# Gate and up products of an encoder layer: sums of weights as additions, two of four made by accumulating transfers

## The chip, the cores and the metric

One core of a Trainium2 chip runs the whole program in one launch. The metric is the device time of one execution in microseconds, lower is better. Engines are named as in the profile: PE is TensorE (matmuls), PEld its weight loads, DVE is VectorE, ACT is ScalarE, POOL is GpSimd, SP is SyncE, which here only issues transfers.

## The reference

One layer of an encoder, applied with the same weights to 512 rows (`x_sample`) and 256 rows (`x_prompt`) of 1024 float32 numbers: a mixer of attention and a gated recurrence, then a gated feed-forward part with a short convolution. The change concerns the first two products of the latter, with weights of 1024 x 2816 each:

```python
def _conv_ffn(xn, w_gate, w_up, conv_w, conv_b, w_down):
    a = xn @ w_gate
    a = lax.conv_general_dilated(a, conv_w[:, None, :], window_strides=(1,),
        padding=((CONV_WIDTH // 2, CONV_WIDTH // 2),),
        dimension_numbers=('NWC', 'WIO', 'NWC'), feature_group_count=D_FF) + conv_b
    b = xn @ w_up
    return (jax.nn.gelu(a, approximate=True) * b) @ w_down
```

## The kernel before

All 768 rows are worked on together. Every float32 operand of a matmul is kept as two float32r parts, a high part (a copy on ScalarE, line 242) and a low part (the difference on VectorE, line 243), and a product is the sum of three matmuls, high by high, high by low, low by high (`split_to`, `product`).

The gate and up products use Strassen's scheme in Winograd's form. The 1024 x 2816 weights are taken in 22 *pairs* p of column tiles: an even p is a tile f of 128 columns of gate and the tile f + 11, an odd p the same tiles of up. A pair is a 2 x 2 matrix of blocks (two halves of the 1024 inputs by the two column tiles), the token rows are halved likewise (2 x 384), and seven products P1 to P7 replace eight. `PRODS` gives their order: P1, P5, P6, P3, P7, P2, P4, each of 4 x 3 matmuls of 128 x 128 by 128 x 384 (`product`, line 857). The sums of token blocks are made once (`ffn_transpose`, lines 792 to 797). The sums of weight blocks are made for each pair: with b11, b21 the two halves of tile f and b12, b22 those of the other tile, P5 needs b12 - b11, P6 that sum taken from b22, P7 needs b22 - b12, P4 the one of P6 taken from b21. They are VectorE operations of 128 x 512 at line 841, written to one of six rotating slots of the buffer `V`.

What each product adds to is fixed by banks of PSUM (`BANK_OF`): P1, P6, P7 and P4 accumulate in one bank, P5 and P3 in a second, P2 has a third; two sets of banks alternate between pairs. In between the bank is read: `keep` (line 873, ScalarE) copies P1, P6 and P5 as they stand, `collect` (line 893, VectorE, and line 889, ScalarE) adds a kept copy to a bank and writes a part of the output. So P6 can only start when P1 has been copied, P3 when P5 has been copied, P4 when the bank has been read after P7. After an even pair follow the convolution (lines 901 to 903) and Gelu (line 904), after an odd pair the multiplication (line 908) and two stores of the gated rows to memory (lines 909 and 910).

The loop of `run` takes products m one after the other: `prep(m)`, `product(m)`, `keep(m)`, `collect(m)`, `prep(m + 6)`. `prep` makes the sum, if the product has one, and splits its weight operand into slot m mod 8 of a ring of eight (`W`), so a split waits until the product eight places earlier is done. At P4 of a pair `prep` also calls `load`, which orders the raw weights of two further tiles on SP (line 228, 512 KB each, five buffers in rotation), the second tile of pair p + 2 and the first of pair p + 3. The first four products in order are P1 and P2 of the first two pairs; then comes the rest of pair 0, pair 1 and so on.

The program is built with `manual_schedule` for SP and POOL: these two queues run in the order of the program text. The order of PE, ACT and DVE is laid down when the program is built and differs from the text (in the trace, ScalarE splits the weights of P3 of the second pair before those of P4 of the first). On the chip every queue runs in its order and waits on semaphores.

Of the kernel before, what the change touches and what calls it, by code (L numbers as in the profile page):

```python
# [10 lines left out]
OP = mybir.AluOpType  # L11
# [7 lines left out]
NF = DFF // 128  # L19
# [15 lines left out]
N_FFN = 40  # L35
# [57 lines left out]
class Encoder:  # L93
# [680 lines left out]
    def ffn_transpose(self, i):  # L774


        nc = self.nc
        b = (3, 5)[TILES.index(i) % 2]
        for k in range(NK):
            nc.tensor.transpose(self.ps[:, b + k // 4, 128 * (k % 4):128 * (k % 4) + 128],  # L780
                                self.v(self.xrow(i) + 128 * k, 128), self.ident)
        t = i % 3
        p1, p2 = self.ps[:, b, :], self.ps[:, b + 1, :]
        r1, r2 = self.V + 1024 * t, self.V + 1024 * t + 512
        if i < 3:
            for name, p, r in (("A11", p1, r1), ("A12", p2, r2)):
                self.operand_split(name, t, p)
                nc.scalar.activation(self.v(r, 512), p, AF.Copy)
            return
        ta, s1 = self.xrow(i), self.xrow(i) + 512  # L790
        nc.scalar.activation(self.v(ta, 512), p2, AF.Copy)
        nc.vector.tensor_tensor(self.v(s1, 512), p1, self.v(ta, 512), op=OP.add)
        self.operand_split("S1", t, self.v(s1, 512))
        nc.vector.tensor_tensor(self.v(ta, 512), self.v(r1, 512), p1, op=OP.subtract)
        nc.vector.tensor_tensor(self.v(r1, 512), self.v(s1, 512), self.v(r1, 512), op=OP.subtract)
        self.operand_split("S2", t, self.v(r1, 512))
        nc.vector.tensor_tensor(self.v(r2, 512), self.v(r2, 512), self.v(r1, 512), op=OP.subtract)
        self.operand_split("S4", t, self.v(r2, 512))
        self.operand_split("S3", t, self.v(ta, 512))
        self.operand_split("A22", t, p2)  # L800
# [26 lines left out]
    def prep(self, upto):  # L827

        nc = self.nc
        while self.n_op < min(upto + 1, len(self.prods)):  # L830
            m = self.n_op
            p, kind = self.prods[m]
            n = N_FFN + 2 * p
            b11, b12 = self.raw(n), self.raw(n if kind in ("P1", "P2") else n + 1)
            b21, b22 = b11 + 512, b12 + 512
            t = [self.V + 512 * ((4 * p + j) % 6) for j in range(4)]
            src, x, y = {"P1": (b11, None, None), "P2": (b21, None, None), "P3": (b22, None, None),
                         "P5": (t[0], b12, b11), "P6": (t[1], b22, t[0]), "P7": (t[2], b22, b12),
                         "P4": (t[3], b21, t[1])}[kind]
            if x is not None:  # L840
                nc.vector.tensor_tensor(self.v(src, 512), self.v(x, 512), self.v(y, 512), op=OP.subtract)
            self.split_to(self.W + 512 * (m % 8), self.W + 4096 + 512 * (m % 8), src, 512)
            self.n_op += 1
            if kind == "P4":
                self.n_split = n + 2
                self.load(n + 7)

    def product(self, m):
        nc = self.nc
        p, kind = self.prods[m]  # L850
        out = self.ps[:, self.pair_banks(p)[BANK_OF[kind]], 0:H]
        xh, xl = self.xop[TOKENS_OF[kind]]
        wh = self.W + 512 * (m % 8)
        wl = wh + 4096
        for k in range(4):
            for wo, xo, first, last in ((wh, xh, True, False), (wh, xl, False, False), (wl, xh, False, True)):
                nc.tensor.matmul(out, self.r(wo + 128 * k, 128), self.r(xo + H * k, H),  # L857
                                 start=kind in BEGINS and k == 0 and first, stop=k == 3 and last, skip_group_check=True)
# [16 lines left out]
    def collect(self, m):  # L875

        nc = self.nc
        p, kind = self.prods[m]
        a, b, c = (self.ps[:, x, 0:H] for x in self.pair_banks(p))
        kept = self.V + 3072 + H * (p % 2)  # L880
        p1, u2, p5 = kept, kept + 2 * H, kept + 4 * H
        C = (self.CG, self.CU)[p % 2]
        bank, add, col, half = {"P2": (c, p1, 0, 0), "P3": (b, u2, 1, 0), "P7": (a, p5, 1, 1),
                                "P4": (a, None, 0, 1)}.get(kind, (None,) * 4)
        if bank is None:
            return
        if add is None:
            for dst, src in self.halves(C + NG * col, lambda x, y: bank[:, x:y], half):
                nc.scalar.activation(dst, src, AF.Copy)
        else:  # L890
            adds = self.halves(C + NG * col, lambda x, y: self.v(add + x, y - x), half)
            for (dst, src), (_, y) in zip(self.halves(C + NG * col, lambda x, y: bank[:, x:y], half), adds):
                nc.vector.tensor_tensor(dst, src, y, op=OP.add)
        f, x = p // 2, {"P7": 1, "P4": 0}.get(kind)
        if x is not None:
            (self.gate if p % 2 == 0 else self.gated)(f + NF // 2 * x, C + NG * x, self.UM + NG * ((2 * f + x) % 4))
# [337 lines left out]
```

## Time and profile before

| | |
|---|---|
| median of 2 runs | 1040.82 us (1038.47 to 1043.16) |
| the profiled execution | 1039.73 us, span from first to last instruction 1037.9 us |
| mean granted clock of TensorE | 0.993 |
| TensorE busy | 997.8 us, 96% of the span |
| VectorE busy | 641.5 us, 62% |
| ScalarE busy | 496.1 us, 48% |
| GpSimd busy | 49.5 us, 5% |
| moved by the DMA engines | 104.04 MB, mean 100 GB/s |

A row of the timeline gives start, duration, engine, line and operation, output and inputs, and in brackets the idle time before it with what ended it. A group gives the number of instructions and their mean. A row of the table of stretches gives the length and, for each engine, busy time and number of instructions, then the granted clock of TensorE (1.00 is full), the mean busy share of the 16 DMA engines, and what they moved. "SPq" is the issue of a transfer on SP.

### The profile page before, as it was taken

To read this page: it belongs to the slowest core of one execution; us is meant where nothing else is said; L and a number is where in the kernel's file an instruction comes from. 1 tells how busy PE (TensorE), PEld (TensorE's weight loads), DVE (VectorE), ACT (ScalarE), POOL (GpSimd) and SP (SyncE) were. 2 spreads that over 40 slices of the span, in tenths; PEclk is the share of its full clock that TensorE was granted. 3 is DMA by queue.
4 is the path that set the end of the run, shared out by engine and by line. 5 is a ranking of instruction groups with operands and counts; after the bars stand their busy time and mean duration, and the time that the engine had idled before them with its cause. 6 is when DMAs were issued, how large, how long until landed. Compare 5 with 4: busy or idle time off the path is not lost.

```text
span 1037.9 us, 19821 instructions
## 1 busy us (share of the span) xinstructions
PE 997.8 (96%) x8239; PEld 889.0 (86%) x8239; DVE 641.5 (62%) x1110; ACT 496.1 (48%) x909; POOL 49.5 (5%) x45
## 2 busy tenths in 40 slices
PE   5998999989999999999989999999999999999997
PEld 5987788778878777679879999999999998888885
DVE  5445748375631776736799778877777773335334
ACT  4362526243232888854656555555445563334321
POOL 1100000000012101000100000000000000000001
PEclk9999999999999999999989999999999999999999
DMA  8041111111023221123335322333323376475413
GB/s 273 19 123 42 43 42 44 42 27 39 23 62 93 61 64 42 51 103 115 120 96 146 112 86 83 101 108 112 112 83 101 105 239 214 163 255 171 127 46 122
DMA packets 109883, 104.04 MB, mean 100 GB/s; under 512 B 4602, under 2 KB 89698, under 8 KB 109794
## 3 DMA queue, kind: packets, MB, share of 16 engines
q1 hardware_dynamic: 108930, 101.21, 31.9%
q8 instruction: 64, 1.05, 0.4%
q10 hardware_dynamic: 864, 1.57, 0.4%
q14 instruction: 25, 0.20, 0.1%
HBM read 85.46 MB, written 14.94 MB: 97 GB/s over the span
## 4 chain that ended last, share of the span: by engine, by line
PE 80%; issue 7%; DVE 6%; ACT 3%; DMA 1%; POOL 1%; SPq 0%; DVEq 0%; POOLq 0%; ACTq 0%
PE ps L857 31%; PE ps L1159 17%; PE ps L338 17%; PE ps L723 4%; PE ps L643 2%; PE ps L430 2%; PE ps L676 2%; PE ps L346 2%; PE ps L665 2%; PE ps L527 1%; DMA RAW<-w_in 1%; DVE S L412 1%; ACT W L242 1%; POOL sm L304 1%; PE ps L524 1%
## 5 line engine op out<-in xcount | busy, mean ns | idle before, releaser
L338 PE MATMUL ps<-X,W 128*128 128x512 f32 (+1 forms) x1200 | 230.4, 342 | 1.3 <-issue 1.3
L338 PEld LDWEIGHTS ps<-X,W 128*128 128x128 f32 x1200 | 185.1, 188 | 28.6 <-issue 3.8
L857 PE MATMUL ps<-XN,W 128*128 128x384 f32 x1056 | 191.7, 339 | 4.7 <-ACT XN L808 4.2
L857 PEld LDWEIGHTS ps<-XN,W 128*128 128x128 f32 x1056 | 186.5, 191 | 6.1 <-ACT XN L808 5.0
L1159 PE MATMUL ps<-W,XN 128*128 128x512 f32 x792 | 179.7, 389 | 0.0
L1159 PEld LDWEIGHTS ps<-W,XN 128*128 128x128 f32 x792 | 148.7, 188 | 30.8
L242 ACT ACTIVATE W<-RAW 128x1024 fp32r<-128x1024 f32 (+1 forms) x92 | 79.6, 868 | 179.5 <-PE ps L338 81.8
L857 PE MATMUL ps<-X,W 128*128 128x384 f32 x792 | 143.2, 338 | 0.0
L857 PEld LDWEIGHTS ps<-X,W 128*128 128x128 f32 x792 | 139.8, 188 | 0.0
L243 DVE TENSOR_TENSOR W<-RAW,W 128x512 fp32r<-128x512 f32 (+1 forms) x82 | 78.1, 955 | 74.6 <-ACT W L242 74.6
L242 ACT ACTIVATE W<-V 128x512 fp32r<-128x512 f32 x88 | 55.2, 629 | 58.6 <-PE ps L857 55.1
L243 DVE TENSOR_TENSOR W<-V,W 128x512 fp32r<-128x512 f32 x88 | 59.7, 687 | 17.8 <-ACT W L242 17.7
L346 PE MATMUL ps<-W,X 128*128 128x256 f32 (+1 forms) x432 | 66.5, 310 | 4.2 <-ACT X L817 2.7
L346 PEld LDWEIGHTS ps<-W,X 128*128 128x128 f32 x432 | 61.4, 194 | 5.9 <-ACT X L817 3.3
L243 DVE TENSOR_TENSOR XN<-X,XN 128x768 fp32r<-128x768 f32 x44 | 41.8, 955 | 35.8 <-ACT XN L242 35.8
L242 ACT ACTIVATE XN<-X 128x768 fp32r<-128x768 f32 x44 | 36.7, 839 | 42.8 <-PE ps L1159 42.1
L723 PE MATMUL ps<-W,X 128*128 128x512 f32 (+1 forms) x288 | 57.1, 343 | 0.0
L723 PEld LDWEIGHTS ps<-W,X 128*128 128x128 f32 x288 | 44.1, 189 | 6.8 <-issue 1.6
L242 ACT ACTIVATE W<-EX 128x512 fp32r<-128x512 f32 (+1 forms) x34 | 25.3, 744 | 46.8 <-PE ps L1159 22.5
L243 DVE TENSOR_TENSOR W<-EX,W 128x512 fp32r<-128x512 f32 (+1 forms) x34 | 28.2, 828 | 29.3 <-ACT W L242 29.3
L304 POOL TENSOR_TENSOR sm<-sm 128x1 f32<-128x1 f32 x24 | 15.2, 641 | 622.8 <-DVE sm L748 588.0
L397 ACT ACTIVATE S<-S 128x384 f32<-128x384 f32 x28 | 15.4, 549 | 46.9 <-PE ps L430 36.6
(187 smaller groups left out, 1159.6 us busy)
## 6 DMA issues: line engine op xcount, KB each, us to landing
X<-gd SPq DMA_DIRECT2D x44, 384.0 KB
RAW<-w_in SPq DMA_DIRECT2D x32, 512.0 KB
RAW<-w_gate SPq DMA_DIRECT2D x14, 512.0 KB
RAW<-w_up SPq DMA_DIRECT2D x13, 512.0 KB
RAW<-w_down SPq DMA_DIRECT2D x13, 512.0 KB
gd<-UM SPq DMA_DIRECT2D x22, 256.0 KB
EX<-w_up SPq DMA_DIRECT2D x9, 512.0 KB
EX<-w_down SPq DMA_DIRECT2D x9, 512.0 KB
```

Of the source, the lines that this page charges most:

```text
L242: nc.scalar.activation(self.r(hi, n), self.v(src, n), AF.Copy)
L243: (eng or nc.vector).tensor_tensor(self.r(lo, n), self.v(src, n), self.v(hi, n), op=OP.subtract)
L304: self.nc.gpsimd.tensor_tensor(r, mean, self.mhalf, op=OP.pow)
L338: nc.tensor.matmul(out, self.r(wo + 128 * k, 128), self.r(xo + T * k + t0, tn), start=(k == 0 and first), stop=(k == NK - 1 and last))
L346: self.nc.tensor.matmul(out, self.r(xo + T * k + 128 * i, 128), self.rap(wo + 128 * k, [[1024, tiles], [1, 128]]), start=(k == 0 and first ...
L430: nc.tensor.matmul(ps[32 * bk:32 * bk + 32, b + h, 32 * c:32 * c + 32], self.v(kt + t0, 32, *HALF[h]), qv(t0, h), start=True, stop=True)
L643: nc.tensor.matmul(ps[:, 4 + h, 0:L], self.r(QS + T * h + t0 + 128 * i, 128), self.r(x + T * h + t0, L), start=z, stop=not z)
L665: nc.tensor.transpose(ps[:, 6 + h, 128 * kt:128 * kt + 128], ms(j, n, h)[:, 128 * kt:128 * kt + 128], self.ident)
L676: nc.tensor.matmul(o[64 * h:64 * h + 64], self.v(vb + 128 * kt + 64 * h, 64), self.v(pt(s, h) + L * kt, L), start=kt == 0, stop=kt == L // ...
L723: nc.tensor.matmul(out, self.r(mo + T * f + 128 * i, 128), rhs, start=(f == 0 and first), stop=(f == NK - 1 and last))
L857: nc.tensor.matmul(out, self.r(wo + 128 * k, 128), self.r(xo + H * k, H), start=kind in BEGINS and k == 0 and first, stop=k == 3 and last, ...
L1159: nc.tensor.matmul(ps[:, banks[half][i], :], self.r(go + 128 * i, 128), self.r(wo_, 512), start=(f == 0 and first), stop=(f == NF - 1 and ...
```

## The change

The sums of weights get other signs, so that each is an addition: P5 uses b12 + b11, P6 adds b22 to it, P7 uses b22 + b12, P4 adds b21 to the one of P6. The sums of token blocks and the collecting of results take the opposite signs in turn. From the second pair on, the sums of P5 and P7 are no longer made by VectorE. A new method `sums(p)` makes them with transfers: two plain ones on SP bring a block of weights (256 KB, runs of 512 bytes) from memory into its slot of `V`, and two on POOL bring another block and add it to what stands there. It is called at the end of `prep` of P4 of pair p - 2 (for pair 1 at P4 of pair 0), behind `load`. The slots of `V` are assigned anew: P5 and P7 have two slots each that alternate between pairs, P6 and P4 one each. For the first pair VectorE makes all four sums as before.

```diff
-        nc.vector.tensor_tensor(self.v(s1, 512), p1, self.v(ta, 512), op=OP.add)
+        nc.vector.tensor_tensor(self.v(s1, 512), p1, self.v(ta, 512), op=OP.subtract)
...
-        nc.vector.tensor_tensor(self.v(r2, 512), self.v(r2, 512), self.v(r1, 512), op=OP.subtract)
+        nc.vector.tensor_tensor(self.v(r2, 512), self.v(r2, 512), self.v(r1, 512), op=OP.add)
...
-            t = [self.V + 512 * ((4 * p + j) % 6) for j in range(4)]
+            t = [self.V + 1024 * (p % 2), self.V + 2048, self.V + 1024 * (p % 2) + 512, self.V + 2560]
+            if p == 0:
+                t = [self.V + 512 * j for j in range(4)]
             src, x, y = {"P1": (b11, None, None), "P2": (b21, None, None), "P3": (b22, None, None),
                          "P5": (t[0], b12, b11), "P6": (t[1], b22, t[0]), "P7": (t[2], b22, b12),
                          "P4": (t[3], b21, t[1])}[kind]
-            if x is not None:
-                nc.vector.tensor_tensor(self.v(src, 512), self.v(x, 512), self.v(y, 512), op=OP.subtract)
+            if x is not None and (p == 0 or kind in ("P6", "P4")):
+                nc.vector.tensor_tensor(self.v(src, 512), self.v(x, 512), self.v(y, 512), op=OP.add)
             self.split_to(self.W + 512 * (m % 8), self.W + 4096 + 512 * (m % 8), src, 512)
             self.n_op += 1
             if kind == "P4":
                 self.n_split = n + 2
                 self.load(n + 7)
+                if p == 0:
+                    self.sums(1)
+                self.sums(p + 2)
+
+    def sums(self, p):
+
+        if p >= NF:
+            return
+        n = N_FFN + 2 * p
+        for x, (n0, k0) in enumerate(((n, 0), (n + 1, 4))):
+            o = self.ap(self.V + 1024 * (p % 2) + 512 * x, [[128, 4], [1, 128]])
+            self.nc.sync.dma_start(o, self.wl[n0][0][:, k0:k0 + 4])
+        for x in range(2):
+            o = self.ap(self.V + 1024 * (p % 2) + 512 * x, [[128, 4], [1, 128]])
+            self.nc.gpsimd.dma_start(o, self.wl[n + 1][0][:, 0:4], accum_op=OP.add)
...
+        op = OP.add if kind == "P2" else OP.subtract
...
             for (dst, src), (_, y) in zip(self.halves(C + NG * col, lambda x, y: bank[:, x:y], half), adds):
-                nc.vector.tensor_tensor(dst, src, y, op=OP.add)
+                src, y = (y, src) if kind == "P7" else (src, y)
+                nc.vector.tensor_tensor(dst, src, y, op=op)
```

## Rows read from the trace of the kernel before

**Rows 1.** The page, first part and chain of lines
```profile
...
PE 997.8 (96%) x8239; PEld 889.0 (86%) x8239; DVE 641.5 (62%) x1110; ACT 496.1 (48%) x909; POOL 49.5 (5%) x45
...
PE ps L857 31%; PE ps L1159 17%; PE ps L338 17%; PE ps L723 4%; PE ps L643 2%; PE ps L430 2%; PE ps L676 2%; PE ps L346 2%; PE ps L665 2%; PE ps L527 1%; DMA RAW<-w_in 1%; DVE S L412 1%; ACT W L242 1%; POOL sm L304 1%; PE ps L524 1%
...
```

**Rows 2.** Table of stretches: 536 to 850, loads of an even pair, two pairs
```profile
...
536.00:850.00 314.00, 314.00 (x1791) 313.78 (x1791) 248.86 (x397) 173.04 (x309) 0.00 (x0) 1.00 0.39 116
649.15:654.00 4.85, 4.85 (x29) 4.85 (x28) 1.59 (x3) 2.02 (x4) 0.00 (x0) 1.00 0.97 280
...
639.80:669.12 29.32, 29.32 (x170) 29.32 (x169) 22.91 (x37) 15.44 (x29) 0.00 (x0) 1.00 0.35 99
...
```

**Rows 3.** Line 841, one of its six forms (nanoseconds min/median/max)
```profile
...
L841 DVE TENSOR_TENSOR V<-RAW,V x27: 681/685/691, 523.4 to 814.4; 128x512 f32<-128x512 f32 x27
...
```

**Rows 4.** Timeline of SP, 648 to 659 us
```profile
...
648.63 0.42 SPq L910 DMA_DIRECT2D gd<-UM  x1
649.15 0.40 SPq L228 DMA_DIRECT2D RAW<-w_gate  x1
649.60 0.69 SPq L228 DMA_DIRECT2D RAW<-w_up  x1
658.72 0.37 SPq L228 DMA_DIRECT2D EX<-w_up  x1
...
```

**Rows 5.** Timeline of all engines, 653 to 671 us
```profile
...
653.40 0.69 DVE L841 TENSOR_TENSOR V<-RAW 128x512 f32<-128x512 f32 x1 [1.81 <-DMA RAW<-w_gate]
...
656.48 8.48 PE L857 MATMUL ps<-XN,W 128*128 128x384 f32 x48
...
657.48 0.62 DVE L893 TENSOR_TENSOR CG<-ps,V 128x128 f32<-128x128 f32 x2
...
659.24 1.01 DVE L902 SCALAR_TENSOR_TENSOR UM<-CG,par,UM 128x768 f32<-128x768 f32 x1
...
660.76 1.01 DVE L903 SCALAR_TENSOR_TENSOR UM<-CG,par,UM 128x768 f32<-128x768 f32 x1
...
662.72 0.69 DVE L841 TENSOR_TENSOR V<-EX,RAW 128x512 f32<-128x512 f32 x1 [0.34 <-DMA EX<-w_up]
662.76 0.83 ACT L904 ACTIVATE UM<-UM 128x769 f32<-128x769 f32 x1
...
663.49 0.47 ACT L873 ACTIVATE V<-ps 128x384 f32<-128x384 f32 x1
...
664.80 6.50 PE L857 MATMUL ps<-X,W 128*128 128x384 f32 x36
...
```

**Rows 6.** Chain in order of time (start, duration), a piece on POOL
```profile
...
301.81 2.27 POOL sm L538
...
```

**Rows 7.** The page's groups: splits of sums, small operations on POOL
```profile
...
L242 ACT ACTIVATE W<-V 128x512 fp32r<-128x512 f32 x88 | 55.2, 629 | 58.6 <-PE ps L857 55.1
L243 DVE TENSOR_TENSOR W<-V,W 128x512 fp32r<-128x512 f32 x88 | 59.7, 687 | 17.8 <-ACT W L242 17.7
...
L304 POOL TENSOR_TENSOR sm<-sm 128x1 f32<-128x1 f32 x24 | 15.2, 641 | 622.8 <-DVE sm L748 588.0
...
```

**Rows 8.** Line 228, 536 to 850 us: who waited for it (us, times)
```profile
...
  DVE V L841: 18.6, 16
...
```

**Rows 9.** Timeline of all engines, 541 to 550 us
```profile
...
541.68 0.68 DVE L841 TENSOR_TENSOR V<-RAW,V 128x512 f32<-128x512 f32 x1
...
542.39 0.37 SPq L228 DMA_DIRECT2D RAW<-w_gate  x1
...
547.93 0.63 ACT L242 ACTIVATE W<-RAW 128x512 fp32r<-128x512 f32 x1 [0.81 <-DMA RAW<-w_gate]
...
548.24 2.38 PE L857 MATMUL ps<-XN,W 128*128 128x384 f32 x12
...
```

**Rows 10.** Table of stretches: around the start of the stage
```profile
...
532.00:535.20 3.20, 0.69 (x1) 0.29 (x1) 3.20 (x7) 1.88 (x3) 0.00 (x0) 0.51 0.00 0
535.20:539.00 3.80, 3.80 (x12) 3.80 (x13) 3.80 (x7) 1.27 (x3) 0.00 (x0) 0.51 0.03 7
...
```

## The prediction, made before the result was known

> **What bounds the kernel now.** I read the page first. TensorE is busy 96% of the span, and the largest part of the chain that ended last, 31% of the span, is line 857, the products of gate and up [rows 1]. Then the table of stretches: between 536 and 850 us TensorE's busy time equals the stretch, 314.00 of 314.00 us, at full granted clock (1.00, so 2.4 GHz), while VectorE is busy 248.86 us (79%), ScalarE 173.04, and the DMA engines 39% [rows 2]. Two pairs repeat every 29.32 us [rows 2]: 2 x 84 matmuls, so 174.5 ns for one, 2.09 us for a product of 12 and 14.66 us for a pair. Nothing in this stage makes TensorE wait. So VectorE time saved here is worth nothing, and the question is only what the new transfers can delay.
>
> **What is removed.** Line 841 runs four times a pair, 0.685 us each [rows 3]. From the second pair on, two of four go (P5, P7): 42 x 0.685 = 28.8 us of VectorE. VectorE is no bound in [rows 2], TensorE covers all of it: 0 us. The turned signs keep number, shape and engine of every instruction in `ffn_transpose`, `prep` and `collect`: 0 us, below nothing too, since an addition and a subtraction differ in nothing the rows show. For the first pair all four sums stay.
>
> **What is added.** Per pair two plain transfers on SP and two accumulating ones on POOL, 256 KB each. The plain ones stand on SP right behind the two 512 KB loads of the same call of `prep`. POOL has nothing else in this stage [rows 2], so its waiting blocks nobody there. SP's two more issues cost 0.4 to 0.7 us each [rows 4] and delay the next store of gated rows, which nobody needs before the down products.
>
> *The chain of one pair's sum.* Take an even pair p, whose loads stand on SP behind the stores of the pair before. In the trace those stores end at 649.05, the loads go out at 649.15 and 649.60 [rows 4], so the first sum's plain transfer would go out at 650.29. The first load is read at 653.40 [rows 5], 4.25 us after its issue. The DMA engines are full meanwhile: 0.97 busy at 280 GB/s [rows 2]. At that rate the second load (524 KB, 1.87 us) lands at 655.3 and the plain 262 KB (0.94 us) at 656.2. Then POOL issues. No row shows POOL issuing a transfer, nor an accumulating one. Bounds for the issue: SP's shortest load issue, 0.37 us [rows 4], and POOL's longest piece of the chain, 2.27 us [rows 6]; I take POOL's mean small operation, 0.64 us [rows 7], as the same engine's. Bounds for the transfer: at best it is a plain one, 4.25 - 1.87 + 0.94 = 3.3 us; at worst it moves each byte like two 512 KB loads one after the other, 8.5 us. I take 4.25, the row of a 512 KB load, since an accumulate has twice the bytes to read. The sum has landed at 656.2 + 0.64 + 4.25 = 661.1 (bounds 659.9 and 667.0).
>
> *What needs it.* P5's split has to find its ring slot free, which is when P1 of the next pair ends on TensorE (656.48 + 3 x 2.1 = 662.7 [rows 5]), and its product is seven products later: 1.6 us of room and 14 us of cover. So the data themselves come in time. But VectorE runs in order, and P6's sum on VectorE reads the accumulated one. That order is fixed when the program is built, from an expected landing time. The trace shows how good such expectations are: VectorE stood idle for loads at line 841 in 16 places, 18.6 us together, 1.2 us each [rows 8], among them the one at 653.40, 1.81 us [rows 5]. The expected landing is early by 1.2 us for one transfer; for load, plain and accumulating transfer in a row I take three times this, 3.5 us (bounds 0, if the order is safe, and three times 1.81, 5.4). P6's sum then stands on VectorE near 657.6 and holds it until 661.1.
>
> *What is late next.* At 657.48 stand the two reads of P7's bank, which free it for P4; P4 starts at 656.48 + 2.1 = 658.6 [rows 5]. If P6's sum is placed ahead of them, they end at 661.1 + 0.69 + 0.62 = 662.4 and TensorE stands still for 3.8 us. If it is placed behind them, the convolution slides (659.24 and 660.76), behind it on ScalarE the second Gelu (662.76) and the copy of P1 (663.49), which frees the bank for P6 of the next pair at 664.80 [rows 5]. A slide of 3.5 us less the room, 1.0 between 661.77 and 662.76 and 0.84 between 663.96 and 664.80, leaves 1.7 us. Between 1.7 and 3.8 I take 3 us, nearer to the first place since 657.6 is within 0.1 us of it. At best it is 0; with the landing at 667.0 and the first place it is 667.0 + 1.3 - 658.6 = 9.7.
>
> For an odd pair the loads go out at 658.72 [rows 4] and the first is read at 662.72 [rows 5]; by the same steps the sum lands at 662.72 + 1.87 + 0.94 + 0.64 + 4.25 = 670.4, and P7 ends only at 664.80 + 6.50 = 671.3: 0 us. There are nine even pairs after the first that order sums (2 to 18): 9 x 3 = 27 us, bounds 0 and 9 x 9.7 = 87.
>
> The Trainium skill (DMA: Bandwidth & Descriptors, section Anatomy of one DMA) gives 2.0 us plus bytes over 436 GB/s for a transfer of POOL's kind, which is 2.6 us for 262 KB as an estimate. By it the sum lands 1.65 us earlier, the stall is 1.3 us or less and the whole term 12 us, so the time 1061; here a 512 KB load on SP takes 4.25 us where that sum gives 3.2, because the engines are full, so I stay with the row.
>
> *The second pair.* Its sums are ordered at P4 of the first pair and are wanted at once. P4's sum runs at 541.68, the loads go out from 542.39 on, the first is read at 547.93, and P5 of the second pair starts on TensorE at 548.24 [rows 9]. With the new chain: second load 549.8, plain sum 550.7, accumulated 555.6, split by ScalarE and VectorE in 0.63 and 0.69 [rows 7], product at 556.9: 8.7 us late. TensorE could take P1 and P2 of the third pair meanwhile (4.2 us), if its order puts them there. Against that, the granted clock fell to 0.51 (its level of 1.2 GHz) for 535.2 to 539, after TensorE had 0.69 us of work in 3.2 [rows 10]; 12 matmuls took 3.8 us there instead of 2.1. I take 9 us (bounds 3, with the fast transfer and the filled gap, and 18, with the slow one, 14.6, and twice the clock's 1.7).
>
> **The sum.** The profiled execution took 1039.73 us (span 1037.9 and 1.8 around it), 1.1 below the median of 1040.82. 1039.7 + 0 (VectorE) + 9 (second pair) + 27 (even pairs) = 1075.7, so 1076.
>
> **The rivals.**
> *Hidden* (not slower). VectorE's order has P6's sum late enough, and only the second pair's start is paid. For it: the data are due 1.6 us and more after the estimated landing, and VectorE is idle a fifth of the stage [rows 2]. Against it: the 16 waits at line 841 stand at the landing itself [rows 8]. It decides from where the landing is less than about 1.8 us behind the expected place. Time: 1039.7 + 9 = 1049.
> *DMA engines become the bound* (slower still). Two pairs now use 0.35 x 29.32 = 10.3 us of the engines [rows 2]; four plain sums add 3.7. That leaves 15.3 us for four accumulating transfers, 3.8 each, four times the plain 0.94. If one takes 5.0, two pairs take 34.0 us instead of 29.3, and ten such spans cost 47: 1039.7 + 9 + 27 + 47 = 1123. Against it: it takes five times the plain price.
> The Trainium skill (same page, section Queues, rings and completion order) says that an engine takes turns between its queues packet by packet, by which accumulating transfers would slow SP's loads rather than wait behind them; no run here shows it yet.
> *Nothing or a gain.* The transfers land early, the gap at the second pair is filled, and the freed VectorE shortens a place outside 536 to 850. The first pair's sums, before which TensorE is idle, are untouched, so there is little to shorten: 1036.
>
> **How the numbers follow.** VectorE held by the sums 0.42 (own range 1055 to 1105), hidden 0.32, DMA bound 0.15, nothing or gain 0.11. Likeliest: 1076. The range 1040 to 1118 leaves out most of the last (0.09) and the upper half of the DMA case (0.09). 2%, about what a measurement of this kernel tells from no change, puts the limits at 1020 and 1061.6. Faster 0.01: TensorE's line leaves no room. Same: hidden 0.32, nothing or gain 0.10, and 0.03 of the first case: 0.45. Slower: 0.39 + 0.15 = 0.54.
>
> **What would show it.** Right: VectorE waits at P6's sum (the line in `prep`) for a transfer on POOL's queue, some 3 us at every even pair; line 857 shows TensorE idle before P4 or P6, released by VectorE's reads or ScalarE's copy of banks; a gap near 548 to 557. The stretch of gate and up products, 314 us now [rows 2], grows by some 36 us. Wrong: line 857 dense as before (hidden), or the DMA share near 1 through the stage (DMA bound). An accumulating transfer that takes under 3 us from issue to landing, or much over 8, would break the chain that I summed.

## The result

The changed kernel takes 1091.93 us (1091.44 and 1092.42) against 1040.82 before, a ratio of 1.050 (95% interval 1.045 to 1.055): 51 us slower. The profiled execution has a span of 1090.7 us, 52.8 more than before.

The page of the changed kernel, its engines, its new queue and its chain by line (line 874 is now the products of gate and up, line 843 the sums on VectorE, 860 the plain and 863 the accumulating transfers, 890 the copies of P1, P6 and P5, 912 the reads of banks on VectorE, 920 to 922 the convolution, 923 Gelu):

```profile
...
PE 1018.1 (93%) x8239; PEld 904.0 (83%) x8239; DVE 619.9 (57%) x1068; ACT 497.0 (46%) x909; POOL 104.1 (10%) x87
...
q0 software_dynamic: 22176, 11.01, 8.2%
...
PE ps L874 20%; PE ps L1178 16%; PE ps L338 16%; DMA V<-w_gate 5%; PE ps L346 3%; PE ps L723 3%; PE ps L643 2%; PE ps L430 2%; PE ps L676 2%; DMA V<-w_up 2%; PE ps L665 1%; DVE W L243 1%; ACT W L242 1%; PE ps L527 1%; DMA RAW<-w_in 1%
...
```

TensorE is down from 96% to 93% of the span and the gate and up products from 31% to 20% of the chain [rows 1]; in their place the chain now runs through transfers into `V` (5% and 2%). The table of stretches, columns as in [rows 2]: two pairs of a usual kind, 6 us around the end of the longest stop, and the stage.

```profile
...
640.41:673.15 32.74, 30.11 (x171) 29.47 (x170) 20.15 (x33) 15.64 (x30) 5.22 (x4) 1.00 0.69 153
...
758.00:764.00 6.00, 3.27 (x10) 3.27 (x11) 4.82 (x7) 4.91 (x9) 2.59 (x2) 0.66 0.51 84
536.00:900.00 364.00, 328.18 (x1765) 322.55 (x1764) 221.58 (x347) 170.38 (x304) 54.70 (x42) 0.95 0.69 158
...
```

Before, TensorE was busy 314.00 of 314.00 us [rows 2]. Now it stands still 364.00 - 328.18 = 35.8 us in 536 to 900. The 1765 matmuls would take 308.0 us at 174.5 ns, and took 328.2: another 20 us go, most of them because the granted clock is at its lower level for part of the time (0.95 in the mean, 0.66 in 758 to 764). The DMA engines are 69% busy, not full. Who waited for whom in the stage (total us, times, longest):

```profile
...
DVE V L843 <- DMA V<-w_gate: 37.7, 9, 6.6
...
PE ps L874 <- ACT V L890: 25.2, 9, 5.0
...
PE ps L874 <- ACT W L242: 6.2, 2, 4.6
...
```

So VectorE waits for the sums of even (gate) pairs, and TensorE waits for ScalarE's copies of banks. (At odd pairs VectorE waits at the same line too, 22.7 us in 7 pieces, which the profile puts down to no transfer; behind them TensorE lost 3.0 us.) How the one becomes the other is seen in one pair, on the timeline of all engines:

```profile
...
640.93 0.41 SPq L228 DMA_DIRECT2D RAW<-w_gate  x1
641.39 0.69 SPq L228 DMA_DIRECT2D EX<-w_up  x1
...
642.17 1.98 SPq L860 DMA_DIRECT2D V<-w_gate  x2
...
648.39 2.61 POOL L863 DMA_DIRECT2D V<-w_gate  x2 [18.46 <-DMA V<-w_gate]
648.46 0.62 DVE L912 TENSOR_TENSOR CG<-V,ps 128x128 f32<-128x128 f32 x2 [0.88 <-PE ps L874]
...
653.06 0.69 DVE L843 TENSOR_TENSOR V<-RAW,V 128x512 f32<-128x512 f32 x1 [3.36 <-DMA V<-w_gate]
653.67 1.01 DVE L921 SCALAR_TENSOR_TENSOR UM<-CG,par,UM 128x768 f32<-128x768 f32 x1
...
655.07 1.01 DVE L922 SCALAR_TENSOR_TENSOR UM<-CG,par,UM 128x768 f32<-128x768 f32 x1
...
656.17 0.85 ACT L923 ACTIVATE UM<-UM 128x769 f32<-128x769 f32 x1 [3.04 <-DVE UM L922]
...
658.42 0.47 ACT L890 ACTIVATE V<-ps 128x384 f32<-128x384 f32 x1
...
658.95 6.61 PE L874 MATMUL ps<-X,W 128*128 128x384 f32 x36 [2.20 <-ACT V L890]
...
```

The loads go out at 640.93, the plain transfers at 642.17, POOL issues at 648.39, and P6's sum on VectorE runs at 653.06, after 3.36 us of waiting for the accumulated one. The reads of P7's bank (648.46) stand ahead of it and are not held up. The convolution stands behind it and is late. With it slide the Gelu (656.17, the first of the pair's two; the prediction calls its counterpart in [rows 5] the second) on ScalarE, the copy of P1 behind that (658.42), and P6 of the next pair on TensorE (658.95), which starts 2.20 us late. Compare [rows 5], where the same chain of convolution, Gelu, copy and product ran with no gap.

How the loss lies over the stage is read from the last store of gated rows of an odd pair, one for each two pairs, first before and then in the changed kernel:

```profile
...
563.12 0.43 SPq L910 DMA_DIRECT2D gd<-UM  x1
...
824.54 0.43 SPq L910 DMA_DIRECT2D gd<-UM  x1
...
```

```profile
...
575.32 1.52 SPq L929 DMA_DIRECT2D gd<-UM  x1
...
607.38 0.42 SPq L929 DMA_DIRECT2D gd<-UM  x1
...
878.20 0.42 SPq L929 DMA_DIRECT2D gd<-UM  x1
...
```

From 575.32 to 878.20 there are nine repeats of two pairs, 33.65 us each, 302.9 together. Before, the same nine took 261.4 (the first only 26.87, the usual one 29.32 [rows 2]): 41.5 us lost. The store of the second pair came 12.2 us later than before, although the first product after the rows' transposes started 2.3 us sooner (531.79, before 534.06): 14.5 us lost in the first two pairs. The tenth repeat, 30.05 us, is 0.3 shorter than before. 14.5 + 41.5 - 2.3 - 0.3 makes 53.4 us, the loss of the stage.

The same two pieces in the table of stretches, before and in the changed kernel, part the loss in another way:

```profile
...
534.06:563.12 29.06, 28.61 (x150) 27.99 (x151) 28.19 (x47) 18.85 (x33) 0.00 (x0) 0.92 0.49 140
563.12:824.54 261.42, 261.42 (x1500) 261.42 (x1499) 204.22 (x329) 137.95 (x251) 0.00 (x0) 1.00 0.35 100
...
```

```profile
...
531.79:575.32 43.53, 34.01 (x157) 32.06 (x158) 29.28 (x47) 20.14 (x35) 8.00 (x6) 0.85 0.75 166
575.32:878.20 302.88, 276.11 (x1494) 272.05 (x1493) 181.53 (x288) 138.02 (x250) 46.70 (x36) 0.95 0.67 149
...
```

TensorE stood still for 9.5 us in the first piece (0.45 before) and 26.8 in the second (0 before), 35.8 us more. And it was busy 310.1 us with what took it 290.0 before, 20.1 more. By the mean clocks some 17 of these are the lower clock (an estimate: 0.15 x 34.0 + 0.05 x 276.1 less 0.08 x 28.6); what the other 3 are is not shown. The lower clock came behind stops, as here, where 36 matmuls that take 6.50 us at full clock [rows 5] took 8.12 and 9.29:

```profile
...
625.63 8.12 PE L874 MATMUL ps<-X,W 128*128 128x384 f32 x36 [1.91 <-ACT V L890]
...
760.73 9.29 PE L874 MATMUL ps<-X,W 128*128 128x384 f32 x36 [4.98 <-ACT V L890]
...
```

### The profile page after: what moved, and what is told of

It reads as the page before. It is cut to its first block, busy times and chain, and to the rows that moved or that the text cites. A ratio compares the mean times of both kernels' runs of the same rounds, so it can differ in the third digit from the quotient of the medians.

```text
span 1090.7 us, 20001 instructions
## 1 busy us (share of the span) xinstructions
PE 1018.1 (93%) x8239; PEld 904.0 (83%) x8239; DVE 619.9 (57%) x1068; ACT 497.0 (46%) x909; POOL 104.1 (10%) x87
## 3 DMA queue, kind: packets, MB, share of 16 engines
q1 hardware_dynamic: 131106, 112.22, 33.9%
## 4 chain that ended last, share of the span: by engine, by line
PE 67%; issue 10%; DVE 8%; DMA 7%; ACT 5%; SPq 1%; POOL 1%; DVEq 0%; POOLq 0%; ACTq 0%
PE ps L874 20%; PE ps L1178 16%; PE ps L338 16%; DMA V<-w_gate 5%; PE ps L346 3%; PE ps L723 3%; PE ps L643 2%; PE ps L430 2%; PE ps L676 2%; DMA V<-w_up 2%; PE ps L665 1%; DVE W L243 1%; ACT W L242 1%; PE ps L527 1%; DMA RAW<-w_in 1%
## 5 line engine op out<-in xcount | busy, mean ns | idle before, releaser
L338 PEld LDWEIGHTS ps<-X,W 128*128 128x128 f32 x1200 | 186.2, 189 | 28.3 <-issue 3.2
L874 PE MATMUL ps<-X,W 128*128 128x384 f32 x792 | 158.4, 362 | 26.8 <-ACT V L890 25.2
L874 PEld LDWEIGHTS ps<-X,W 128*128 128x128 f32 x792 | 152.9, 206 | 30.2 <-ACT V L890 28.3
L243 DVE TENSOR_TENSOR XN<-X,XN 128x768 fp32r<-128x768 f32 x44 | 41.8, 955 | 35.8 <-ACT XN L242 35.7
L863 POOL DMA_DIRECT2D V<-w_gate x20 | 27.0, 1590 | 178.8 <-DMA V<-w_gate 140.8
```

The lines of the kernel that those rows point to most:

```text
L243: (eng or nc.vector).tensor_tensor(self.r(lo, n), self.v(src, n), self.v(hi, n), op=OP.subtract)
L863: self.nc.gpsimd.dma_start(o, self.wl[n + 1][0][:, 0:4], accum_op=OP.add)
```

## The experiments

Four things could cost these 53 us: the order of VectorE (theory A: the engine runs in order and meets P6's sum too early), the transfers' bytes on the DMA engines (rival B), the new slots and signs (rival C), or the accumulation itself, by which a transfer lands later (rival D). All kernels ran beside the kernel before, and the ratios are to it.

**No transfers: slots and signs alone, and the relief alone.** The first kernel makes all four sums on VectorE:

```diff
-            if x is not None and (p == 0 or kind in ("P6", "P4")):
+            if x is not None:
...
-                if p == 0:
-                    self.sums(1)
-                self.sums(p + 2)
```

> The changed kernel's signs and slots of V, but all four sums of a pair on VectorE and no transfers for them. Theory A (VectorE runs in order and waits at P6's sum for the accumulated one) and rival B (the transfers themselves are too slow or load the DMA engines, whatever the order) both expect the time of the kernel before, 1041 us within 4. Rival C (the new slots, one each for P6 and P4 instead of six in rotation, hold the pairs back) expects 1070 or more.

1041.4 us, ratio 1.0001 (0.9985 to 1.0018). The slots and the signs cost nothing; rival C falls. The second leaves out the sums of P5 and P7 altogether:

```diff
+            if p and kind in ("P5", "P7"):
+                src = x
+            if p and kind == "P6":
+                y = b12
...
-                if p == 0:
-                    self.sums(1)
-                self.sums(p + 2)
```

> The sums of P5 and P7 are left out from the second pair on, by VectorE and by transfers alike (their products use one block of the two), so that part of the computation is missing. This is the change with transfers that cost nothing. If VectorE time is worth nothing in this stage, 1041 us within 4; if it were worth its 28.8 us, 1012.

1041.3 us, ratio 1.0014 (0.9994 to 1.0035). Its stretch, as in [rows 2]:

```profile
...
536.00:850.00 314.00, 314.00 (x1793) 313.60 (x1792) 227.41 (x353) 172.56 (x308) 0.00 (x0) 1.00 0.40 118
...
```

VectorE has 227.41 us of work instead of 248.86, TensorE is as full as before. This is the most that the change could have brought: nothing.

**The order of VectorE alone.** One edit to the changed kernel: the code of every transfer is as it was, and P6's sum is laid behind the last operation of an earlier pair's convolution or multiplication. The build moves some splits and convolutions on VectorE and ScalarE by a few places with it; TensorE's order stays.

```diff
             if x is not None and (p == 0 or kind in ("P6", "P4")):
-                nc.vector.tensor_tensor(self.v(src, 512), self.v(x, 512), self.v(y, 512), op=OP.add)
+                with (self.tc.issue_after(self.late) if kind == "P6" and self.late else __import__("contextlib").nullcontext()):
+                    nc.vector.tensor_tensor(self.v(src, 512), self.v(x, 512), self.v(y, 512), op=OP.add)
...
-        nc.vector.scalar_tensor_tensor(self.v(u, T), self.v(c + 1, T), w[2], self.v(u, T), op0=OP.mult, op1=OP.add)
+        i = nc.vector.scalar_tensor_tensor(self.v(u, T), self.v(c + 1, T), w[2], self.v(u, T), op0=OP.mult, op1=OP.add)
+        self.late = i.ins
...
-        nc.vector.tensor_tensor(self.v(u, T + 1), self.v(u, T + 1), self.v(c, T + 1), op=OP.mult)
+        i = nc.vector.tensor_tensor(self.v(u, T + 1), self.v(u, T + 1), self.v(c, T + 1), op=OP.mult)
+        self.late = i.ins
...
+        self.late = None
```

> The changed kernel with one edit: on VectorE the sum of P6 is placed behind the convolution (or the multiplication) of the pair before the last, all transfers as they are. The repeat of two pairs took 32.9 us in the changed kernel instead of 29.3, ten times, so 36 of its 51 us. Theory A expects these back: 1056 us (1050 to 1062), with line 912 and 921 no longer behind a wait for a transfer. Rival B and rival C expect 1088 to 1095, as the transfers and slots are the same.

1055.77 us, ratio 1.0155 (1.0123 to 1.0187): 36 us back, as theory A had it. (The 32.9 us of the expectation is too small, the nine repeats took 33.65.) The nine repeats (574.98 to 840.95) give back 36.9 of 41.5 us. Timeline (line 923 is the convolution's second operation here, 844 the sum, 864 the accumulating transfer):

```profile
...
612.28 2.59 POOL L864 DMA_DIRECT2D V<-w_gate  x2 [20.13 <-DMA V<-w_gate]
...
620.75 1.02 DVE L923 SCALAR_TENSOR_TENSOR UM<-CG,par,UM 128x768 f32<-128x768 f32 x1
621.69 0.69 DVE L844 TENSOR_TENSOR V<-EX,V 128x512 f32<-128x512 f32 x1
...
```

The accumulated sum is ordered at 612.28 as in the changed kernel, 7.5 us after the load (604.75), and VectorE comes to P6's sum at 621.69, 9.4 us after the order, and does not wait. The stretch of 600 to 650 us:

```profile
...
600.00:650.00 50.00, 50.00 (x289) 50.00 (x288) 33.65 (x53) 26.43 (x50) 7.80 (x6) 1.00 0.77 178
...
```

TensorE is full again with the DMA engines at 77%, more than in the changed kernel. Rival B, the bytes as a bound of the stage, falls with this row; at the stage's opening they still count (below). Two later repeats are 0.6 and 1.5 us longer, behind waits of ScalarE for an accumulated sum at the split of P5 (1.40 us before 679.60, 2.31 before 739.77).

**Ordering the sums earlier.** The order of VectorE is left to the build, and from the second pair on the transfers go out behind P7's split, ahead of the loads.

```diff
                 if p == 0:
                     self.sums(1)
+                    self.sums(2)
+            if p and kind == "P7":
                 self.sums(p + 2)
```

> The changed kernel with its sums ordered earlier: from the second pair on, the call stands behind P7's split instead of behind P4's and its loads, so that the plain transfers go out ahead of the two 512 KB loads. The order of VectorE is left to the build. Theory A expects the landing some 4 to 6 us sooner at even pairs and most of the 36 us back: 1056 to 1068 us. Rival B (load on the DMA engines) expects 1088 or more, since the same bytes move; rival C the same as the changed kernel.

1061.2 us, ratio 1.0197 (1.0170 to 1.0223). The time is inside theory A's range, but its reason is not borne out: VectorE's waits for the sums hardly shrank.

```profile
...
DVE V L843 <- DMA V<-w_gate: 34.1, 8, 5.7
...
```

34.1 us in 8 pieces, before 37.7 in 9. When the transfer is ordered sooner, the build also places the sum sooner: near 645 it stands ahead of the reads of P7's bank, the convolution follows in time, and P6 of the next pair starts without a stop. The nine repeats of two pairs take 29.7 us each here, so most of the 21 us that this kernel loses lie in the first two pairs, whose store comes at 578.79 instead of 563.12. Two kernels with nearly the same waits thus lose 0.7 and 4.6 us a repeat: what a wait costs is set by what is queued behind it, not by its length.

**The price of accumulating.** The transfers on POOL stay, without the addition.

```diff
-            self.nc.gpsimd.dma_start(o, self.wl[n + 1][0][:, 0:4], accum_op=OP.add)
+            self.nc.gpsimd.dma_start(o, self.wl[n + 1][0][:, 0:4])
```

> The changed kernel with the accumulating transfers on POOL turned into plain ones of the same bytes: the addition in P5's and P7's sums is left out. It prices the accumulation. If reading back and adding is what makes the sums late (rival D), they land 2 us sooner or more and the time is 1075 or less. If it is the place at the end of a chain of three transfers and POOL's issue of 1.3 us (theory A), the time stays within 8 us of the changed kernel's: 1084 to 1095.

1068.49 us, ratio 1.0282 (1.0266 to 1.0297): 23 us less than the changed kernel, so here theory A's expectation failed and rival D's held (in the time; the landing came 1.9 us sooner where it had 2). The issues on POOL (those out of `w_up` and out of `w_gate`, nanoseconds min/median/max) and the time from issue to landing, of the changed kernel and then of this one:

```profile
...
L863 POOL DMA_DIRECT2D V<-w_up x22: 1282/1636/1852, 549.3 to 866.3; - x22
L863 POOL DMA_DIRECT2D V<-w_gate x20: 1282/1332/2951, 551.0 to 854.1; - x20
...
DMA to landing us min/median/max: 4.4/5.4/10.5
```

```profile
...
L863 POOL DMA_DIRECT2D V<-w_up x22: 747/747/917, 549.7 to 842.0; - x22
L863 POOL DMA_DIRECT2D V<-w_gate x20: 747/747/756, 551.4 to 832.4; - x20
...
DMA to landing us min/median/max: 3.2/3.5/7.8
```

Accumulating makes the issue on POOL longer, from 0.75 us to 1.28 and more, and the landing 1.9 us later in the median (5.4 against 3.5). VectorE's waits for even pairs fall from 37.7 to 26.6 us and the repeat of two pairs from 33.65 to 31.35 us. Both readings are true at once: the chain is too long for the place that P6's sum has, and the accumulation is the part of it that makes up nearly half of the loss. With the order mended, the same accumulation cost nothing in the row of 600 to 650 above.

**Half the transfers.** The plain ones on SP stay, VectorE adds the second block.

```diff
-            if x is not None and (p == 0 or kind in ("P6", "P4")):
+            if p and kind in ("P5", "P7"):
+                x, y = src, x if kind == "P5" else y
+            if x is not None:
...
-        for x in range(2):
-            o = self.ap(self.V + 1024 * (p % 2) + 512 * x, [[128, 4], [1, 128]])
-            self.nc.gpsimd.dma_start(o, self.wl[n + 1][0][:, 0:4], accum_op=OP.add)
```

> The plain transfers on SP stay, the accumulating ones go: VectorE adds the second block in place, so that four sums a pair are again on VectorE, two of them fed by the plain transfers. Theory A expects that the chain without POOL's step ends near enough to where VectorE's order has it: 1045 us (1040 to 1052). Rival B (bytes on the DMA engines) expects about half the loss, 1060 to 1070.

1045.83 us, ratio 1.0061 (1.0042 to 1.0080). A chain without POOL's step is nearly where VectorE's order expects it: the waits for transfers of even pairs come to 0.5 us each. (About half of the 6 us above the kernel before lie ahead of the stage, whose first product starts at 537.19 instead of 534.06.)

```profile
...
DVE V L845 <- DMA V<-w_gate: 4.4, 9, 1.1
...
```

**The start.** First the second pair's sums on VectorE, all else as in the changed kernel:

```diff
-            if x is not None and (p == 0 or kind in ("P6", "P4")):
+            if x is not None and (p <= 1 or kind in ("P6", "P4")):
...
-                if p == 0:
-                    self.sums(1)
```

> The changed kernel, but VectorE also makes all four sums of the second pair, so that transfers begin with the third. What is left of the 51 us beside ten repeats of two pairs, 15 us, is laid to the second pair's sums being ordered only when they are wanted (9 us in the prediction). Theory A expects 1077 us (1073 to 1083). If the 15 us have another cause in the stage, 1088 or more.

1090.03 us, ratio 1.0493 (1.0477 to 1.0510): not the 1077 expected. The stores of gated rows show what became of it:

```profile
...
569.51 0.42 SPq L927 DMA_DIRECT2D gd<-UM  x1
...
600.35 0.42 SPq L927 DMA_DIRECT2D gd<-UM  x1
...
877.24 0.42 SPq L927 DMA_DIRECT2D gd<-UM  x1
...
```

The second pair's store comes at 569.51, 5.8 us sooner than in the changed kernel, that of the fourth at 600.35, 7.0 sooner. From there to 877.24 the repeats take 34.6 us each (33.9 in the changed kernel over the same eight), and the gain is given back. The order is laid anew in each build, so this run does not isolate the start. The next does, since it has the order mended too (in its expectation, the run before is the one with VectorE's order alone, and the count of sums is muddled: 40 of 88 are gone from VectorE):

> Both cures together, VectorE's order as in the run before and the second pair's four sums on VectorE; from the third pair on the transfers are those of the changed kernel. If the two causes are all there is, 1042 us (1038 to 1047), the time of the kernel before with 80 of 88 - 42 VectorE sums gone and nothing gained. A cause that is still missing leaves it above 1050.

1050.27 us, ratio 1.0105 (1.0086 to 1.0123), 5.5 us less than with the order alone; 8 us above the 1042 expected. The two places, ScalarE and TensorE of one of them (line 889 copies P6, 873 is the product), and the stretch after them:

```profile
...
558.56 0.63 ACT L242 ACTIVATE W<-V 128x512 fp32r<-128x512 f32 x1 [4.77 <-DMA V<-w_gate]
...
561.25 0.47 ACT L889 ACTIVATE V<-ps 128x384 f32<-128x384 f32 x1
...
561.78 3.92 PE L873 MATMUL ps<-X,W 128*128 128x384 f32 x12 [4.74 <-ACT V L889]
...
```

```profile
...
600.00:850.00 250.00, 250.00 (x1434) 250.00 (x1433) 173.91 (x272) 131.10 (x240) 41.54 (x32) 1.00 0.77 176
...
```

ScalarE waits 4.77 us at the split of P5 for the accumulated sum, the copy that stands behind it comes at 561.25, and TensorE stood still for 4.74 us. It happens once more near 588 (ScalarE waits 4.10 us, TensorE 2.05), and after 600 never again: 250.00 of 250.00 us. The likely reason is seen in the stretch from POOL's issue to that second landing, beside the same place of a later repeat (the share of the DMA engines can pass 1 because the shares of two queues are added):

```profile
...
581.00:588.20 7.20, 6.16 (x36) 5.83 (x34) 2.17 (x3) 3.06 (x7) 4.09 (x4) 1.00 1.26 246
609.00:617.00 8.00, 8.00 (x48) 8.00 (x47) 5.08 (x10) 5.30 (x9) 2.59 (x2) 1.00 0.72 160
...
```

The even pair's loads went out at 572.00 and the odd pair's already at 578.02, ahead of POOL's issue at 581.12; in the later repeat the odd pair's come 8.8 us after the even pair's and behind POOL's issue. There the sum took 7.0 us to land (5.6 in the median of this run) while the DMA engines were full, and at the first stop, 551.90 to 558.60, the share is 1.26 as well. In the two runs that follow the same edits are kept (e8 is this run, e3 the one with the order alone). One also orders the sums earlier, as above, the other leaves all sums up to the fifth pair to VectorE (`p <= 4` and, for the call, `p > 2`):

> Order of VectorE and second pair as in e8, and from the second pair on the sums ordered behind P7's split, ahead of the loads. In e8 TensorE stood still twice (4.7 and 2.1 us near 557 and 587) because ScalarE, also in order, waited 4.8 and 4.1 us at the split of P5 for the accumulated sum; after 600 it never did. The theory that the rest is ScalarE's wait for sums that are late in the opening burst of loads expects these sums some 4 us sooner from the fourth pair on, so the second stop goes: 1043 to 1048 us. If the rest is the bytes on the DMA engines, 1050 again.

> Order of VectorE as in e3 and e8, but VectorE makes all sums up to the fifth pair; the transfers begin with the sixth, when the opening burst is over. The same theory expects no wait at all: 1041 us (1038 to 1043). If transfers that have just begun always cost some 10 us (a first use of POOL's queue, say), 1048 to 1052.

They gave 1046.53 us, ratio 1.0046 (1.0032 to 1.0059), and 1039.78 us, ratio 0.9985 (0.9971 to 0.9999). Sooner transfers take away the second stop (one wait of ScalarE is left, 5.6 us); beginning after the opening takes away both. So the rest of the loss was ScalarE's wait for sums that are late while the DMA engines still carry the loads of the stage's opening. The stretch of the last kernel:

```profile
...
536.00:850.00 314.00, 313.44 (x1792) 312.61 (x1791) 231.64 (x362) 172.44 (x307) 44.33 (x34) 1.00 0.74 174
...
```

34 of the 42 accumulating transfers are left, and all run in it; VectorE has 231.64 us of work, TensorE 313.44 of 314.00. From its first product to the first of the down products the stage takes 318.0 us (532.09 to 850.12), before 317.2 (534.06 to 851.22). No version gained anything that 2% could tell from the kernel before, which the second experiment had said beforehand.

## Why the prediction came true, and where it was short

*What bounds, and the worth of the relief.* Right: TensorE's line left no room, and the run without these sums took 1.0014 of the time before. The signs and slots at 0 us: 1.0001.

*The chain of one sum.* From the first load's issue to P6's sum I had 661.1 - 649.15 = 12.0 us; it took 653.06 - 640.93 = 12.1. POOL's issue came 7.5 us after the load (I had 7.0), and 4.7 us later the sum was there (4.9). The issue on POOL was under-sized, 1.28 us at the least instead of 0.64, and the transfer in this pair over-sized by about as much; that the two cancel is luck. The Trainium skill's sum for a transfer of POOL's kind (DMA: Bandwidth & Descriptors, Anatomy of one DMA), 2.6 us as an estimate, is 0.9 short of the plain ones measured (3.5) and 2.8 short of the accumulating ones in the median (5.4), for which the page gives no figure of their own; had I gone by it, the forecast would have been 1061.

*The wait.* 3.5 us expected, 3.36 in the pair shown; over the nine even pairs 37.7 / 9 = 4.2. That three times the wait for one transfer comes so near is luck too: no row bore out the factor.

*The place.* It was the second of my two: behind the reads of P7's bank, ahead of the convolution. I had 1.7 us of stop for it and took 3 as a mean with the other; the pair shown has 2.20.

*The stops of even pairs.* 27 us forecast; TensorE stood still for 26.8 us in the nine repeats, of which 1.6 belong to odd pairs, where I had 0. That the size fits is luck in part: 3 was a mean of two places, of which only the second occurred, and there longer waits, 6.1 and 5.7 us in two of nine, cost 4.98 and 4.57 instead of 1.7. In the first repeat ScalarE, too, waited 4.69 us for the sum, at the split of P5 (591.64). So "the data themselves come in time" holds in the changed kernel from there on, and not before.

*The second pair.* 9 us forecast; TensorE stood still for 9.5 us up to that pair's store, against 0.45 before. The sum itself was on time (ScalarE's split at 553.84, 13.7 us after the load at 540.15; by my steps 555.6 - 542.39 = 13.2).

*The clock* is the term that was missing. With the stops at 36 us as summed, TensorE also took 20 us longer for the same matmuls: 4 in the first two pairs and 16 in the nine repeats (seven matmuls that moved from these to those counted at 174.5 ns), most of it at the lower clock. For the even pairs I had put this at nothing, though [rows 10] show the clock at 0.51 after a stop; for the second pair it stood in the upper bound alone.

*The rivals.* Hidden fell because the order was not safe; with the order made so, the kernel came near it (1055.77, forecast 1049). The DMA engines were no bound: 69% busy in the changed kernel, 77% in a stretch without any loss. The queue of the accumulating transfers took 8.2% of 16 engines' span, 0.082 x 1090.7 / 42 = 2.1 us for one, where that rival needed more than 3.8. A gain was not there to be had, as the run without the sums shows. The rule of the Trainium skill that a DMA engine takes turns between its queues (DMA: Bandwidth & Descriptors, Queues, rings and completion order) was not needed for the result; no run here shows it.

So 1076 was forecast and 1092 measured, slower as forecast. The mechanism was right, its size was 16 us short: the 20 us by which the matmuls took longer, less some 2 by which the stage began sooner and about 2 in small differences.

## What to carry to other kernels

Work taken off an engine that is not the bound is worth nothing, so look first at what the new supplier adds: a chain of transfers has to be set against the place that its first consumer has on its engine, and behind that consumer against whatever the bound engine needs next. An engine that runs in order turns a late input of a step that nobody needs soon into a stop of the steps behind it; pinning that step behind the urgent ones cost a few lines here and gave 36 of 51 us back. Where the bound engine stops, count also what the clock does behind each stop: here that was some 17 us (the estimate above) beside 36 of standing still. At the opening of a stage, where loads come in a burst, the same chain was later than in its steady run (7.0 us to land where the run's median is 5.6), and beginning it some repeats in took away the last 10 us of the loss.

## What the runs showed of the hardware

An accumulating transfer of 256 KB on POOL took 1.28 us and more to issue and 5.4 us from issue to landing in the median, a plain one of the same shape 0.75 and 3.5. Of the DMA engines' time it took 2.1 us (8.2% of the span for 42 of them). 32 of them in 250 us, with the DMA engines 77% busy, cost TensorE nothing.

In a stage that is otherwise full, a stop of TensorE could cost more than its length. In six of the nine repeats (stops of 1.83 to 4.98 us) the product behind the stop ran partly at the lower clock: 36 matmuls took 8.1 to 9.3 us instead of 6.5, 24 of them 7.2. In the other three (1.84 to 2.20 us) they took 6.6. What decides between the two no run here shows. The repeat with the stop of 4.98 us took 37.3 us instead of 29.3.
